# First stage with weight pieces ahead, norm chain in three pieces, gate rows into the convolution's tiles: one change to a hybrid decoder layer on one core

## Chip, cores and metric

The kernel runs on one core of a Trainium2 chip. The metric is the device time of one execution in microseconds. Engines are TensorE (PE; its weight loads are PEld), VectorE (DVE), ScalarE (ACT), GpSimd (POOL) and SyncE (SP); DMAs are issued from the queues of SP, ACT and POOL.

## What is computed

One decoder layer over 2048 tokens of width 1024, in float32, and a final RMSNorm:

```python
shift, scale, gate = split(c @ w_ada + b_ada, 3)
h = rmsnorm(x, g_pre) * (1 + scale) + shift
p = h @ w_in                       # 8 groups of 1024 columns
a = p[A_VAL] * sigmoid(p[A_GLU])
y = causal_depthwise_conv31(a, conv_w) + conv_b
y = silu(layernorm(y, conv_ln_g, conv_ln_b)) * silu(p[A_SILU])
y_a = y @ w_conv_out
u, v = gelu(p[B_U]), layernorm(gelu(p[B_V]), sgu_ln_g, sgu_ln_b)
s = per_head_causal_128x128_mix(w_s, v) + b_s
y_b = (u * s * silu(p[B_SILU])) @ w_sgu_out
merged = sigmoid(p[G_A]) * y_a + sigmoid(p[G_B]) * y_b
x = x + gate * (merged @ w_o)
out = rmsnorm(x, g_final)
```

## The kernel before

Tokens are worked in two stages of S = 1024, each in two halves of T = 512; KT = 8 tiles of 128 cover the width and NC = 4 tiles of 128 tokens a half. Float32 products are made of three matmuls: each operand is split into a first part (rounded, made by ScalarE) and a second part (the difference, made by VectorE or POOL), and first times first, first times second and second times first are added. A weight's two parts lie in a tile `whl` (5 buffers), made from a `raw` tile (8 buffers, loaded by SP). `split` (L87, L88) does it; `take` hands the pieces out in a fixed list `order` and prepares AHEAD = 4 of them. Such a piece is 128x512 in both parts; a matmul takes 128 weight columns against 512 columns.

**First stage, written by hand (L511 to L627).** Under a manual schedule each engine runs its instructions in the order written. The transposed x of the first 512 tokens is loaded into `xn`, squared on ACT (L535), summed on DVE (L536) and by TensorE (L143), and the reciprocal root, spread over all partitions by a matmul of `ones` with a diagonal (L150, L164), scales h. Then eight steps follow, one per 128 rows of the weight `w_v`. In step k TensorE runs 24 matmuls for the v columns (L592, L593, L597; the last step is L605 to L607), while for step k+1 VectorE computes the modulation (`ada`, L434), scales xn (L374), makes the second parts of two weight pieces (L88) and of h (L390), and ScalarE makes h's first part (L380) and the first parts of the weights (L87). ScalarE also squares the second half's tokens (`sx`, L585) in steps 5 and 6, takes the root (L136), loads the Gelu table by a call on one element (`warm`, L600), and evicts v (L562). In step 7 a second spread (L611) gives the second half's reciprocal root `rx1`.

The pass over the second half's v (L320 to L322) follows. From here on the tile scheduler orders instructions by priority; `run_bg(n)` puts n steps of a background list `bg` between TensorE's products at a later priority, `urgent` at the normal one, and `pause(n)` puts n empty steps in. Then come position mixing (L478), and 28 `quad`s, each a 2x2 block product of w_in in seven multiplications (L305, L308, L311). VectorE runs the convolution's taps beside them (L766, in `y` tiles of tag `x`, 8 buffers).

**Norm chain.** In background: the mean (L878), for each half eight `centre` steps (subtraction L886, square L891, adding up L895), `ln_cols` (four column sums L143, root L136, reciprocal L137), `ln_spread` (diagonal L150, matmul L164, copy to `rsq` L905). `conv_out` uses it (L941 to L944).

**Products with w_b and w_a** follow in `std_pairs`, a quarter of the columns at a time: a quarter is two halves by two columns, a product of 24 matmuls each. `done_b` multiplies by a loaded gate in its `ld` buffer (3 of them) and stores from there on POOL's queue. In the first token stage, `gate_step` (L979 to L991) loads 16 half rows of `wgate` into `raw` tiles and accumulates them on DVE in `acc`, beside the products with w_a. After these, the output product, the residual and, in the last stage, the final norm and the stores. The next stage's x is loaded (L350) into `x` tiles.

## Time and profile before

| | |
|---|---|
| runs | 1900.91, 1895.69, 1900.12 us; median 1900.12 |
| profiled execution | 1895.41 us |
| its span | 1893.7 us |
| mean granted clock of TensorE | 0.994 |
| TensorE busy | 1837.6 us, 97 %, 8104 matmuls |
| TensorE's weight loads busy | 1502.4 us, 79 % |
| VectorE busy | 1326.2 us, 70 %, 1608 instructions |
| ScalarE busy | 854.5 us, 45 % |
| GpSimd busy | 876.0 us, 46 % |
| DMA | 316.28 MB, mean 167 GB/s |

The profile is one execution, recorded by the hardware; its own time is 1895.41 us, of which the span, first to last instruction, is 1893.7. Busy times of the engines overlap. A timeline gives the start, the duration, the engine, the line, the operation with its tiles (out<-in), how many were put together (x4) and, in brackets, how long the engine had been idle before and which engine's result (or which DMA) ended that. A row whose engine ends in q is a queue's issuing work. A granted clock of 1.0 is TensorE's full level, 2.4 GHz; 0.50 is 1.2 GHz.

### The profile page before, as it was taken

To read this page: it belongs to the slowest core of one execution; us is meant where nothing else is said; L and a number is where in the kernel's file an instruction comes from. 1 tells how busy PE (TensorE), PEld (TensorE's weight loads), DVE (VectorE), ACT (ScalarE), POOL (GpSimd) and SP (SyncE) were. 2 spreads that over 40 slices of the span, in tenths; PEclk is the share of its full clock that TensorE was granted. 3 is DMA by queue.
4 is the path that set the end of the run, shared out by engine and by line. 5 is a ranking of instruction groups with operands and counts; after the bars stand their busy time and mean duration, and the time that the engine had idled before them with its cause. 6 is when DMAs were issued, how large, how long until landed. Compare 5 with 4: busy or idle time off the path is not lost.

```text
span 1893.7 us, 23201 instructions
## 1 busy us (share of the span) xinstructions
PE 1837.6 (97%) x8104; PEld 1502.4 (79%) x8104; DVE 1326.2 (70%) x1608; ACT 854.5 (45%) x1392; POOL 876.0 (46%) x734
## 2 busy tenths in 40 slices
PE   6899999999999999899999999999999999999998
PEld 4678888888888778678888888888888886888886
DVE  6887789888889854465852578778888798534424
ACT  3745455555546653222612455455555466412102
POOL 0156777777777620101100677777777776110000
PEclk9999999999999999999999999999999999999999
DMA  9673333232333277776885423233322233954494
GB/s 350 215 266 108 104 112 112 96 105 73 112 107 111 101 298 257 262 229 233 339 306 191 160 97 100 74 117 106 117 95 96 82 134 123 335 176 139 135 345 164
DMA packets 139733, 316.28 MB, mean 167 GB/s; under 512 B 15968, under 2 KB 16096, under 8 KB 139616
## 3 DMA queue, kind: packets, MB, share of 16 engines
q1 hardware_dynamic: 108576, 238.60, 37.2%
q0 software_dynamic: 11888, 41.43, 5.6%
q10 hardware_dynamic: 19152, 34.78, 4.9%
q8 instruction: 63, 1.03, 0.2%
q14 instruction: 54, 0.44, 0.1%
HBM read 229.28 MB, written 85.46 MB: 166 GB/s over the span
## 4 chain that ended last, share of the span: by engine, by line
PE 75%; issue 9%; DMA 6%; DVE 4%; ACT 2%; POOL 2%; SPq 0%; ACTq 0%; POOLq 0%; DVEq 0%
PE bank L305 22%; PE bank L311 22%; PE bank L308 22%; PE bank L320 3%; PE bank L322 3%; PE bank L321 3%; DMA raw<-in_w_v 1%; PE bank L478 1%; DMA wo<-d_wo 1%; DVE a L941 1%; DMA raw<-in_wgate 1%; ACT whl L87 1%; DMA xn<-in_xt 1%; DVE rsq L895 1%; POOL whl L88 1%
## 5 line engine op out<-in xcount | busy, mean ns | idle before, releaser
L88 POOL TENSOR_TENSOR whl<-raw,whl 128x512 fp32r<-128x512 f32 x392 | 523.4, 1340 | 339.0 <-ACT whl L87 334.2
L766 DVE SCALAR_TENSOR_TENSOR cv<-a,vec,cv 128x1024 f32<-128x1024 f32 x464 | 597.0, 1287 | 31.5 <-ACT cv L760 21.4
L87 ACT ACTIVATE whl<-raw 128x512 fp32r<-128x512 f32 x504 | 314.7, 627 | 389.2 <-PE bank L311 224.5
L311 PE MATMUL bank<-s,whl 128*128 128x512 f32 x896 | 351.9, 393 | 0.0
L305 PE MATMUL bank<-s,whl 128*128 128x512 f32 x896 | 351.5, 392 | 0.0
L308 PE MATMUL bank<-s,whl 128*128 128x512 f32 x896 | 350.1, 391 | 0.0
L232 POOL TENSOR_TENSOR raw<-raw 128x512 f32<-128x512 f32 x224 | 295.4, 1319 | 17.3
L305 PE MATMUL bank<-h,whl 128*128 128x512 f32 x672 | 264.0, 393 | 1.7 <-ACT bank L719 1.7
L308 PE MATMUL bank<-h,whl 128*128 128x512 f32 x672 | 262.4, 390 | 0.0
L311 PE MATMUL bank<-h,whl 128*128 128x512 f32 x672 | 261.7, 389 | 0.0
L311 PEld LDWEIGHTS bank<-s,whl 128*128 128x128 f32 x896 | 169.4, 189 | 36.3 <-issue 1.0
L305 PEld LDWEIGHTS bank<-s,whl 128*128 128x128 f32 x896 | 169.3, 189 | 36.4 <-issue 1.5
L308 PEld LDWEIGHTS bank<-s,whl 128*128 128x128 f32 x896 | 169.2, 189 | 35.6 <-issue 0.5
L305 PEld LDWEIGHTS bank<-h,whl 128*128 128x128 f32 x672 | 126.1, 188 | 33.8 <-DVE snap L742 5.7
L311 PEld LDWEIGHTS bank<-h,whl 128*128 128x128 f32 x672 | 126.2, 188 | 27.0 <-issue 0.5
L308 PEld LDWEIGHTS bank<-h,whl 128*128 128x128 f32 x672 | 126.2, 188 | 26.0 <-issue 0.5
L88 DVE TENSOR_TENSOR whl<-raw,whl 128x512 fp32r<-128x512 f32 x112 | 75.9, 688 | 60.0 <-ACT whl L87 59.4
L970 POOL DMA_DIRECT2D mb<-gl x32 | 17.3, 541 | 199.5 <-DVE gl L969 199.5
L714 ACT ACTIVATE snap<-bank 128x512 f32<-128x512 f32 x112 | 66.4, 597 | 94.3 <-PE bank L311 93.6
L311 PE MATMUL bank<-ya,whl 128*128 128x512 f32 x256 | 100.5, 392 | 5.4 <-DVE whl L88 5.3
L305 PE MATMUL bank<-ya,whl 128*128 128x512 f32 x256 | 100.2, 391 | 1.0 <-ACT whl L87 1.0
L305 PE MATMUL bank<-yb,whl 128*128 128x512 f32 x256 | 99.8, 390 | 1.0 <-ACT whl L87 1.0
(212 smaller groups left out, 2852.2 us busy)
## 6 DMA issues: line engine op xcount, KB each, us to landing
raw<-in_w_in SPq DMA_DIRECT2D x224, 256.0 KB, 3.0
yb<-yb SPq DMA_DIRECT2D x32, 512.0 KB, 8.0
whl<-d_wo SPq DMA_DIRECT2D x32, 512.0 KB, 4.7
whl<-d_wv SPq DMA_DIRECT2D x32, 512.0 KB, 4.2
wa<-in_wada SPq DMA_DIRECT2D x16, 512.0 KB, 7.8
raw<-in_w_v SPq DMA_DIRECT2D x32, 256.0 KB, 6.0
d_wv<-whl POOLq DMA_DIRECT2D x16, 512.0 KB, 6.6
r<-r POOLq DMA_DIRECT2D x32, 256.0 KB, 3.2
```

The costliest lines, as they stand in the source:

```text
L87: nc.scalar.activation(hi, val, AF.Copy)
L88: eng.tensor_tensor(out=lo, in0=val, in1=hi.bitcast(F32), op=ALU.subtract)
L232: eng.tensor_tensor(out=dst, in0=dst, in1=src, op=ALU.add)
L305: nc.tensor.matmul(pt, wh, h[:, 0], start=start and k == 0, stop=False, skip_group_check=True)
L308: nc.tensor.matmul(pt, wh, h[:, 1], start=False, stop=False, skip_group_check=True)
L311: nc.tensor.matmul(pt, wl, h[:, 0], start=False, stop=k == last, skip_group_check=True)
L320: nc.tensor.matmul(pt, xh, w[:, 0], start=kt == 0, stop=False)
L321: nc.tensor.matmul(pt, xh, w[:, 1], start=False, stop=False)
L322: nc.tensor.matmul(pt, xl, w[:, 0], start=False, stop=kt == KT - 1)
L478: nc.tensor.matmul(pq[:, c * P : (c + 1) * P], vn[c][:, j * P : (j + 1) * P], wsT[:, j * P : (j + 1) * P], start=c == 0, stop=True, skip_g ...
L714: nc.scalar.activation(t, pt, AF.Copy)
L766: nc.vector.scalar_tensor_tensor(out=dst, in0=a[:, k : k + S], scalar=col(V_CW, j * TAPS + k), in1=cv[0], op0=ALU.mult, op1=ALU.add,)
```

## The change

1. First loads: the first two tiles of x go on ACT's queue and the other six on SP's, in place of every second on ACT's.
2. First stage: `pieces_hi` (ACT) makes the first parts of step k+1's weights before h's first part; `pieces_lo` (DVE) makes the second parts after h's scaling. The rows of `w_v` for this pass leave `order`.
3. The squares of `sx`, the root and the Gelu table's call are issued inside the steps, ahead of h's first part; only the reciprocal and the diagonal remain behind the steps.
4. Norm chain: `ln_cols`, `ln_diag` and `ln_spread` are background steps of their own. Three `centre` steps of the second half stand ahead of the first half's sums, three between sums and diagonal, two and a pause between diagonal and spread, and pauses ahead of the second half's sums, diagonal and spread. Both stages use it.
5. `done_b` writes its product to a new t512 tile `mb`; the `ld` tile is free once read.
6. Gate rows: eight loads of whole rows (128x1024, 512 KB) on POOL's queue into `x` tiles, in which the convolution was, and eight accumulations of 128x1024 on DVE, behind a pause of 16 steps and with pauses of 2 between them. The next stage's x tiles wait for the end of the accumulation (L1154 of after; before it was for `rsq`).
7. The last stage's stores: second halves of the columns on ACT's queue, not SP's.

The diff, with unchanged lines and the pure renaming cut:

```diff
@@ -155,11 +155,10 @@
-    def spread(cols, pt=None, diag=None):
-        diag = diagonal(cols) if diag is None else diag
+    def spread(diag, pt=None):
         pt = bank() if pt is None else pt
@@ -261,7 +260,6 @@
         if s == 0:
-            order += [make_row(w_v, None, k, n) for k in range(KT) for n in range(2)]
             order += [make_row(w_v, d_wv, k, n) for n in range(2) for k in range(KT)]
@@ -512,7 +510,7 @@
         for k in range(KT):
-            (nc.scalar if k % 2 else nc.sync).dma_start(
+            (nc.scalar if k < 2 else nc.sync).dma_start(
                 out=xn[k][:, :T], in_=xt[k * P : (k + 1) * P, :T]
@@ -542,10 +540,26 @@
         ada_part(0, 0, wa[0])
-        prx = spread(rstd_cols(pc[:, :NC], NC), pc)
+        prx = spread(diagonal(rstd_cols(pc[:, :NC], NC)), pc)
         ada_part(0, 1, wa[0])
         rx = t512("rx")
-        prep_to(2)
+        pieces = {}
+        def pieces_hi(k):
+            pieces[k] = [piece_tile() for _ in range(2)]
+            for n in range(2):
+                nc.scalar.activation(pieces[k][n][:, 0], raws[id(w_v), k, n], AF.Copy)
+        def pieces_lo(k):
+            for n in range(2):
+                w = pieces[k][n]
+                nc.vector.tensor_tensor(
+                    out=w[:, 1], in0=raws.pop((id(w_v), k, n)), in1=w[:, 0].bitcast(F32),
+                    op=ALU.subtract,
+                )
+        pieces_hi(0)
+        pieces_lo(0)
         scaled(xn, prx, 0, 0)
@@ -556,6 +570,9 @@
+        def square(c):
+            nc.scalar.activation(sx[c], sx[c], AF.Square, accum_out=ssx[:, c : c + 1])
         def evict(u):
@@ -564,8 +581,7 @@
             t = A[0][k]
-            ws = [ready.pop(0) for _ in range(2)]
-            state["use"] += 2
+            ws = pieces[k]
             if k + 4 < KT:
@@ -574,17 +590,20 @@
             if k + 1 < KT:
+                pieces_hi(k + 1)
+                if k in (5, 6):
+                    square(2 * k - 10)
+                    square(2 * k - 9)
+                if k == 6:
+                    c1 = sm.tile([P, NC], F32, tag="ro", name="c1")
+                    nc.scalar.activation(c1, ssx, AF.Sqrt, bias=eps_t, scale=1.0 / D)
+                    nc.scalar.activation(warm, eps_t, AF.Gelu)
                 ada(k + 1, wa[k + 1])
...
                 h_hi(xn, 0, k + 1, A)
-                prep_to(2 * k + 4)
+                pieces_lo(k + 1)
                 h_lo(xn, 0, k + 1, A)
                 shifted(xn, 0, k + 1)
-            if k in (5, 6):
-                for c in (2 * k - 10, 2 * k - 9):
-                    nc.scalar.activation(
-                        sx[c], sx[c], AF.Square, accum_out=ssx[:, c : c + 1]
-                    )
             if k + 1 < KT:
@@ -595,9 +614,8 @@
                     nc.tensor.matmul(first[u], xl, ws[n][:, 0], start=False, stop=False)
-        c1 = rstd_cols(ssx, NC)
+        nc.vector.reciprocal(out=c1, in_=c1)
         diag1 = diagonal(c1)
-        nc.scalar.activation(warm, eps_t, AF.Gelu)
         rx1 = t512("rx1")
@@ -608,7 +626,7 @@
                 evict(1)
-                nc.scalar.activation(rx1, spread(c1, None, diag1), AF.Copy)
+                nc.scalar.activation(rx1, spread(diag1), AF.Copy)
                 scaled(xn, rx1, 1, 0)
@@ -867,6 +885,7 @@
         rcols = [None, None]
+        rdiag = [None, None]
         ya = [[None] * KT, [None] * KT]
@@ -900,8 +919,11 @@
+        def ln_diag(h):
+            rdiag[h] = diagonal(rcols[h])
         def ln_spread(h):
-            pr = spread(rcols[h], stat[0][:, half(h)])
+            pr = spread(rdiag[h], stat[0][:, half(h)])
             nc.scalar.activation(rsq[0][:, half(h)], pr, AF.Copy)
@@ -911,13 +933,19 @@
         pause(1)
-        for h in range(2):
-            bg.extend(lambda h=h, j=j: centre(h, j) for j in range(KT))
-            if h:
-                bg.append(urgent(lambda: ln_spread(0)))
-            else:
-                pause(2)
-            bg.append(urgent(lambda h=h: ln_cols(h)))
+        bg.extend(lambda j=j: centre(0, j) for j in range(KT))
+        steps = [lambda j=j: centre(1, j) for j in range(KT)]
+        bg.extend(steps[:3])
+        bg.append(urgent(lambda: ln_cols(0)))
+        bg.extend(steps[3:6])
+        bg.append(urgent(lambda: ln_diag(0)))
+        bg.extend(steps[6:])
+        pause(2)
+        bg.append(urgent(lambda: ln_spread(0)))
+        pause(2)
+        bg.append(urgent(lambda: ln_cols(1)))
+        pause(3)
+        bg.append(urgent(lambda: ln_diag(1)))
         pause(4)
@@ -965,9 +993,9 @@
         def done_b(j, h, pt):
-            g = load(d_sbg[j][h], "gl")
-            nc.vector.tensor_tensor(out=g, in0=pt, in1=g, op=ALU.mult)
-            nc.gpsimd.dma_start(out=d_mb[j][h], in_=g)
+            g, m = load(d_sbg[j][h], "gl"), t512("mb")
+            nc.vector.tensor_tensor(out=m, in0=pt, in1=g, op=ALU.mult)
+            nc.gpsimd.dma_start(out=d_mb[j][h], in_=m)
@@ -976,21 +1004,27 @@
-            def gate_step(r, n):
-                t = raw(wgate, None, wgate[r * P : (r + 1) * P, n * T : (n + 1) * T])
-                if not acc:
+            wg = []
+            for r in range(KT):
+                wg.append(xtile("wg")[:, :S])
+                nc.gpsimd.dma_start(out=wg[r], in_=wgate[r * P : (r + 1) * P, :])
+            def gate_step(r):
+                if r == 0:
                     acc.append(row("acc"))
-                v = acc[0][:, n * T : (n + 1) * T]
-                if r == 0:
                     nc.vector.tensor_scalar(
-                        out=v, in0=t, scalar1=col(V_C, r), scalar2=None, op0=ALU.mult
+                        out=acc[0], in0=wg[0], scalar1=col(V_C, 0), scalar2=None, op0=ALU.mult
                     )
...
                     nc.vector.scalar_tensor_tensor(
-                        out=v, in0=t, scalar=col(V_C, r), in1=v, op0=ALU.mult, op1=ALU.add
+                        out=acc[0], in0=wg[r], scalar=col(V_C, r), in1=acc[0],
+                        op0=ALU.mult, op1=ALU.add,
                     )
-            bg.extend(lambda r=r, n=n: gate_step(r, n) for r in range(KT) for n in range(2))
+            pause(16)
+            for r in range(KT):
+                bg.append(lambda r=r: gate_step(r))
+                pause(2)
         mg = [[None] * KT, [None] * KT]
@@ -1108,7 +1142,7 @@
                         nc.scalar.activation(o, o, AF.Copy, scale=rs)
-                    nc.sync.dma_start(
+                    (nc.scalar if n else nc.sync).dma_start(
                         out=out[t0 : t0 + P, n * T : (n + 1) * T], in_=o
@@ -1119,7 +1153,7 @@
         for k in range(KT):
-            after(xn[k][:, 0:1], rsq[0][:, 0:1])
+            after(xn[k][:, 0:1], acc[0][:, S - 1 : S])
         for h in range(2):
@@ -1128,7 +1162,7 @@
             after(r[:, 0:1], came)
-            nc.scalar.activation(r, spread(rs_next[h]), AF.Copy)
+            nc.scalar.activation(r, spread(diagonal(rs_next[h])), AF.Copy)
             rxs.append(r)
```

How the change moves instructions, at three places. In the rows, `h` is h's tile, `whl` a weight's pieces, `xn` the scaled x, `sx` the second half's tokens, `vn` the evicted v, `cols` and `c_626` the column of roots, `a` the convolution's tile (y), `rsq` the spread root, `q` a square, `zl` a loaded factor. Numbers behind names tell tiles apart; L numbers are each kernel's own.

ScalarE, from step 5 of the first stage to its first evictions, before:

```order
L380 ACTIVATE h<-xn,mod 128x512
L87 ACTIVATE whl<-raw 128x512 x2
L380 ACTIVATE xn<-xn,mod 128x512
L585 ACTIVATE sx,ssx<-sx 128x1024 x2
L380 ACTIVATE h<-xn,mod 128x512
L87 ACTIVATE whl<-raw 128x512 x5
L380 ACTIVATE xn<-xn,mod 128x512
L585 ACTIVATE sx,ssx<-sx 128x1024 x2
L136 ACTIVATE cols<-ssx,eps_t 128x4
L600 ACT_TABLE_LOAD
L600 ACTIVATE warm<-eps_t 128x1
L562 ACTIVATE vn<-bank 128x512 x2
```

and in the changed kernel:

```order
L551 ACTIVATE whl<-raw 128x512 x2
L574 ACTIVATE sx,ssx<-sx 128x1024 x2
L378 ACTIVATE h<-xn,mod 128x512
L378 ACTIVATE xn<-xn,mod 128x512
L551 ACTIVATE whl<-raw 128x512 x2
L574 ACTIVATE sx,ssx<-sx 128x1024 x2
L87 ACTIVATE whl<-raw 128x512
L599 ACTIVATE c_626<-ssx,eps_t 128x4
L600 ACT_TABLE_LOAD
L600 ACTIVATE warm<-eps_t 128x1
L378 ACTIVATE h<-xn,mod 128x512
L87 ACTIVATE whl<-raw 128x512 x2
```

Behind each pair of weight pieces (L87 before, L551 after) the squares now follow ahead of h's first part (L380, L378), and root and Gelu table (L599, L600) stand ahead of the last h instead of behind everything.

VectorE, in the pass over the second half's v, around the second part of the pass's first weights, `whl_799`, before:

```order
L390 SCALAR_TENSOR_TENSOR h_731<-xn_222,mod_86,h_731 128x512
L390 SCALAR_TENSOR_TENSOR h_736<-xn_223,mod_86,h_736 128x512
L390 SCALAR_TENSOR_TENSOR h_741<-xn_224,mod_86,h_741 128x512
L374 SCALAR_TENSOR_TENSOR xn_225<-xn_225,mod_86,rx1_666 128x512
L374 SCALAR_TENSOR_TENSOR xn_226<-xn_226,mod_86,rx1_666 128x512
L466 BN_AGGR mv_757<-st_233 128x2
L466 BN_AGGR mv_757<-st_234 128x2
L466 BN_AGGR mv_757<-st_235 128x2
L88 TENSOR_TENSOR whl_799<-raw_800,whl_799 128x512
L390 SCALAR_TENSOR_TENSOR h_746<-xn_225,mod_86,h_746 128x512
L390 SCALAR_TENSOR_TENSOR h_751<-xn_226,mod_86,h_751 128x512
```

and in the changed kernel:

```order
L372 SCALAR_TENSOR_TENSOR xn_224<-xn_224,mod_86,rx1_666 128x512
L372 SCALAR_TENSOR_TENSOR xn_225<-xn_225,mod_86,rx1_666 128x512
L372 SCALAR_TENSOR_TENSOR xn_226<-xn_226,mod_86,rx1_666 128x512
L388 SCALAR_TENSOR_TENSOR h_741<-xn_224,mod_86,h_741 128x512
L388 SCALAR_TENSOR_TENSOR h_746<-xn_225,mod_86,h_746 128x512
L388 SCALAR_TENSOR_TENSOR h_751<-xn_226,mod_86,h_751 128x512
L464 BN_AGGR mv_757<-st_233 128x2
L464 BN_AGGR mv_757<-st_234 128x2
L464 BN_AGGR mv_757<-st_235 128x2
L88 TENSOR_TENSOR whl_799<-raw_800,whl_799 128x512
L88 TENSOR_TENSOR whl_805<-raw_806,whl_805 128x512
L88 TENSOR_TENSOR whl_823<-raw_824,whl_823 128x512
```

`whl_799` stands behind the last two h's (`h_746`, `h_751`), which followed it before, and the next two second parts follow it directly.

VectorE, in the first token stage's norm chain, behind the first half's spread and up to the second spread's diagonal, before:

```order
L895 TENSOR_TENSOR rsq_5082<-rsq_5082,q_5326 128x512
L941 TENSOR_TENSOR a_1216<-a_1216,rsq_5082 128x512
L941 TENSOR_TENSOR a_1758<-a_1758,rsq_5082 128x512
L941 TENSOR_TENSOR a_2214<-a_2214,rsq_5082 128x512
L941 TENSOR_TENSOR a_2672<-a_2672,rsq_5082 128x512
L941 TENSOR_TENSOR a_3129<-a_3129,rsq_5082 128x512
L137 RECIPROCAL cols_5355<-cols_5355 128x4
L941 TENSOR_TENSOR a_3586<-a_3586,rsq_5082 128x512
L941 TENSOR_TENSOR a_4043<-a_4043,rsq_5082 128x512
L941 TENSOR_TENSOR a_4500<-a_4500,rsq_5082 128x512
L150 TENSOR_TENSOR diag_5415<-ident_80,cols_5355 128x512
L943 TENSOR_TENSOR a_1216<-a_1216,zl_5699 128x512
```

and in the changed kernel:

```order
L969 TENSOR_TENSOR a_1758<-a_1758,rsq_5082 128x512
L969 TENSOR_TENSOR a_2214<-a_2214,rsq_5082 128x512
L971 TENSOR_TENSOR a_1216<-a_1216,zl_5700 128x512
L971 TENSOR_TENSOR a_1758<-a_1758,zl_5708 128x512
L969 TENSOR_TENSOR a_2672<-a_2672,rsq_5082 128x512
L969 TENSOR_TENSOR a_3129<-a_3129,rsq_5082 128x512
L969 TENSOR_TENSOR a_3586<-a_3586,rsq_5082 128x512
L969 TENSOR_TENSOR a_4043<-a_4043,rsq_5082 128x512
L971 TENSOR_TENSOR a_2214<-a_2214,zl_5716 128x512
L969 TENSOR_TENSOR a_4500<-a_4500,rsq_5082 128x512
L137 RECIPROCAL cols_5394<-cols_5394 128x4
L150 TENSOR_TENSOR diag_5435<-ident_80,cols_5394 128x512
```

The reciprocal (L137) stood between the fifth and sixth product of y with the first half's spread (L941) and the diagonal (L150) behind all eight; now both stand behind the eighth (L969), and three products with `zl` (L971) have moved ahead of them.

## Rows read from the trace of the kernel before

**Rows 1.** What TensorE waited for: tile, line, releaser: us in total, times, longest.

```profile
PE cv L164 <- DVE diag L150: 9.4, 4, 3.0
PE bank L311 <- DVE whl L88: 5.3, 1, 5.3
PE bank L164 <- ACT vn L562: 3.3, 1, 3.3
PE bank L305 <- ACT whl L87: 2.0, 3, 1.0
...
PE bank L321 <- DVE whl L88: 1.6, 1, 1.6
...
PE bank L320 <- ACT vn L460: 1.0, 1, 1.0
```

**Rows 2.** Windows at half clock: length, PE, PEld, DVE, ACT, POOL busy, clock, DMA, GB/s.

```profile
72.40:75.80 3.40, 2.84 (x5) 1.61 (x6) 1.60 (x4) 1.72 (x5) 0.00 (x0) 0.50 1.01 381
635.60:639.00 3.40, 3.40 (x10) 2.72 (x11) 2.55 (x5) 0.26 (x1) 1.45 (x2) 0.50 0.21 74
666.30:673.10 6.80, 5.88 (x12) 3.97 (x13) 4.82 (x8) 3.30 (x6) 1.29 (x1) 0.50 0.25 77
799.40:802.80 3.40, 2.95 (x7) 2.38 (x8) 3.02 (x6) 0.00 (x0) 0.32 (x1) 0.50 0.72 240
1594.70:1598.10 3.40, 3.03 (x5) 1.81 (x6) 1.81 (x4) 0.92 (x2) 0.00 (x0) 0.50 0.30 80
```

**Rows 3.** Timeline of TensorE, first stage: start, us, engine, line, operation.

```profile
28.08 0.39 PE L592 MATMUL bank<-whl,h 128*128 128x512 f32 x1
...
31.48 0.39 PE L593 MATMUL cv<-whl,h 128*128 128x512 f32 x1
...
72.96 2.07 PE L164 MATMUL bank<-diag,ones 128*128 128x512 f32 x2 [3.35 <-ACT vn L562]
```

**Rows 4.** Timeline of VectorE, one step of the first stage.

```profile
41.19 1.22 DVE L434 CUSTOM_DVE_ANT_0 wa<-wa,cbc 128x1024 f32<-128x1024 f32 x1
...
45.92 1.29 DVE L88 TENSOR_TENSOR whl<-raw,whl 128x512 fp32r<-128x512 f32 x2 [1.31 <-ACT whl L87]
...
47.80 1.22 DVE L434 CUSTOM_DVE_ANT_0 wa<-wa,cbc 128x1024 f32<-128x1024 f32 x1
```

**Rows 5.** Timeline of ScalarE, end of the first stage.

```profile
58.48 1.14 ACT L87 ACTIVATE whl<-raw 128x512 fp32r<-128x512 f32 x2
...
69.45 1.04 ACT L585 ACTIVATE sx<-sx 128x1024 f32<-128x1024 f32 x1
...
70.92 1.28 ACT L600 ACT_TABLE_LOAD   x1
72.22 0.20 ACT L600 ACTIVATE warm<-eps_t 128x1 f32<-128x1 f32 x1
```

**Rows 6.** Timeline of VectorE, pass over the second half.

```profile
85.22 2.10 DVE L390 SCALAR_TENSOR_TENSOR h<-xn,mod,h 128x512 fp32r<-128x512 f32 x3
...
88.83 0.64 DVE L88 TENSOR_TENSOR whl<-raw,whl 128x512 fp32r<-128x512 f32 x1
```

**Rows 7.** Timeline of VectorE, norm chain, behind the first spread.

```profile
656.20 6.39 DVE L941 TENSOR_TENSOR a<-a,rsq 128x512 f32<-128x512 f32 x5 [1.25 <-ACT rsq L905]
```

**Rows 8.** Timelines of VectorE and of SyncE's queue, gate rows and next x.

```profile
797.71 0.49 DVE L985 TENSOR_SCALAR acc<-raw,vec 128x512 f32<-128x512 f32 x1 [8.64 <-DMA raw<-in_wgate]
...
889.61 0.15 DVE L92 COPY rx<-mg 128x1 f32<-128x1 f32 x1
...
786.96 3.27 SPq L350 DMA_DIRECT2D xn<-in_xt  x5
...
793.21 6.33 SPq L177 DMA_DIRECT2D raw<-in_wgate  x5
```

**Rows 9.** Window within the steps of the first stage, columns as in rows 2.

```profile
27.90:39.30 11.40, 11.23 (x50) 8.92 (x48) 8.66 (x16) 4.47 (x8) 0.00 (x0) 1.00 1.03 401
```

**Rows 10.** DMA issues: queue, number, KB each, us from issue to landing.

```profile
d_wv<-whl POOLq DMA_DIRECT2D x16, 512.0 KB, 6.6
```

## Prediction, before the change was run

> **What bounds the kernel now.** Read the busy shares first: TensorE is busy 97 % of the 1893.7 us span, VectorE 70 %. Little can come from giving other engines less to do; what can be won is time in which TensorE stands still or runs slowly. So the second view is the list of what TensorE waited for, where nearly every long entry is one place waiting for one engine [rows 1]. The third is the clock: in windows where TensorE's granted clock was 0.50, the 1.2 GHz level in place of 2.4 GHz, every busy microsecond does half a microsecond's work, so half of its busy time is lost [rows 2]. Each of these windows follows a wait of over 1.5 us or a string of column sums. The fourth is the timeline of the first stage, where no single wait is long and yet TensorE is slow: between two steps it idles in many small pieces that the waits list hardly shows [rows 3 to 5].
>
> **First stage.** In full flow a matmul takes, from start to start over 15 of them, (31.48 − 28.08)/15 = 0.2267 us [rows 3], so a step's 24 matmuls need 5.44 us. But one step lasts 47.80 − 41.19 = 6.61 us, counted on VectorE, and 1.31 us of that is VectorE waiting until ScalarE has made the first parts of the weights [rows 4]. Before, ScalarE makes them only after h's first part; now it makes them ahead of it, as the first order listing shows, and the wait should go. VectorE is then left with 6.61 − 1.31 = 5.30 us a step, just under TensorE's 5.44, so TensorE paces the steps. Step 1 begins at 28.08 [rows 3], so step 7 can begin at 28.08 + 6 × 5.44 = 60.7.
>
> The spread for the second half of tokens stands within step 7. Before, it is issued at 72.96, after a wait of 3.35 us [rows 3], because four squares of 1.04 us and the Gelu table (1.28 us) stand at the end of ScalarE's work, two squares after step 7's own pieces [rows 5]. The change puts squares, square root and table ahead of h's first part of steps 6 and 7. They are not free there: from the end of step 5 (28.08 + 5 × 5.44 = 55.3), which frees the next pieces' tiles, ScalarE must run two pieces (1.14), two squares (2.08), the root and its gap (0.4), the table (1.28) and its warming call (0.20) [rows 5], then h's first part, of a piece's size (0.57): in all 5.7 us, so h comes at about 61.0, 0.3 behind TensorE. Its second part takes VectorE about as long, seven more matmuls 1.6, and with the hand-overs the spread is issued at about 63.5. **The stage gives 72.96 − 63.5 = 9.45 us**; between 7.5 (a residue of 0.3 on each of six steps) and 10.0 (ScalarE hidden wholly).
>
> A rule speaks against putting the table into the step. The rows show the load at 70.92 for 1.28 us and the warming call at 72.22, 0.02 us behind it: the switch costs 1.3 us [rows 5]. The Trainium skill ("ScalarE: Activation LUTs", section "What ACT_TABLE_LOAD costs") adds a drain of about 1.38 us to each switch, which would put h's first part as much later and the gain at about 8.1. This trace disagrees, and I take the rows.
>
> The first loads of x, four and four on the queues of ScalarE and SyncE, become two and six. No row prices it; the nearest are SyncE's issues, from 3.27/5 = 0.65 to 6.33/5 = 1.27 us each [rows 8]. ScalarE is spared two issues and SyncE has two more, so −1.3 to +1.3; as ScalarE has the squares of these tiles to do and SyncE the loads behind, I take −0.3.
>
> **Pass over the second half.** VectorE does about 16 us of work between the spread and the second part of the pass's first weights, which before starts at 88.83 [rows 6]. The second order listing shows that piece now behind two more h's (0.70 each [rows 6]), while the step that is done before it is shorter: some +0.4 us, measured from the spread. This stretch hangs on VectorE, so the 1.42 us that the slow clock at 72.40 costs is not won: TensorE only arrives earlier, and its wait of 1.6 [rows 1] grows to 3 or 4. After such a wait I expect a new stretch of slow clock (+1.7, half of a window of 3.40 us [rows 2]; likely, not sure); the later wait of 1.0 for vn [rows 1] is covered by the delay. **Net +0.9**, between −0.8 and +2.1.
>
> **Norm chain, both stages.** TensorE waits 9.4 us in four spreads, the longest 3.0 [rows 1]. Counting rows in TensorE's order, 67 matmuls stood between the first half's sums and its spread, now 48; but squares and subtractions of the second half no longer stand between the sums and the diagonal: nine VectorE instructions at 0.64 are some 6 us, against 48 × 0.2267 = 10.9. For the second spread, 24 + 48 matmuls and two spreads of 1 us each stand after the first one, 18.3 us, where 4 + 30 stood. VectorE needs, by the third listing, eight products at 6.39/5 = 1.28 [rows 7], three more at 0.64, a reciprocal and the diagonal (0.9), with the 1.25 us of waiting ahead [rows 7] and ScalarE's copy about 15 us. Both margins hold. **−8.4**, with 1.0 kept for what is late next; ends −9.4 and −3.0. The mean's and column sums' own order costs nothing: VectorE's three earlier subtractions (1.9 us) lie under nine more matmuls (2.04).
>
> **Slow clock.** The five windows hold 2.84 + 3.40 + 5.88 + 2.95 + 3.03 = 18.10 us busy, 9.05 lost [rows 2]. Without the one counted in the pass (1.42), and with an even chance that the one behind the column sums at 635.60 stays (0.85), **−6.8**; ends −1.5 (only the one at the gate rows goes) and −9.05.
>
> **Gate rows.** Before, VectorE stands 8.64 us for a raw load of the gate weights [rows 8], and a weight's second part is queued behind it; TensorE waits 5.3 for that piece, and 2.0 for ScalarE pieces that use the same raw buffers [rows 1]. Now the rows come on POOL's queue into tiles of the convolution, ahead of use by a pause of 16 steps, in eight operations of 128x1024. **−6.3**, with 1.0 kept; ends −7.3 and, with loads that come late (below), +6.6. What is queued behind a load that waits for its tile is a store of the merge product, in POOL's queue; that product now has a buffer of its own, so the loaded one is free at its read. The next stage's loads of x, issued from 786.96 on before, now wait for the accumulations, which share their tiles; VectorE first makes a tile ready for their use at 889.61 [rows 8], four quarters later, so this costs 0. The last stores share two queues: an issue is at most 1.27, either way; I take 0.
>
> **Sum.** −0.3 − 9.45 + 0.9 − 8.4 − 6.8 − 6.3 = −30.35. The profiled execution took 1895.41; so 1865.1 for one like it. The median of the runs, 1900.12, stands 4.7 above it. I add half, 2.35: **1867 us**.
>
> **Rivals.** *Second spread stays late.* For it: products of 128x512 take 1.28 there [rows 7], twice the 0.64 of another on VectorE [rows 6], and if its other operations took as long, the margin of 3.3 us would be used up. Against it: TensorE has twice the matmuls. Two waits of 3.0 and half of their windows' 5.88 + 3.03 return: +10.5, 1877. *The loads pace the first stage.* In 27.90 to 39.30 the DMA share is 1.03 at 401 GB/s [rows 9]. A step moves 1.57 MB, 3.9 us at this pace, less than 5.44; but requests bunch. Half of the steps' gain, 4.7 us, would stay away: 1872. *Gate loads a little late*: four of the eight in file (by the next rival's prices 4 × 7.82 − 21.8 = +9.5) and two slow windows behind them (3.4): 1877 to 1880.
>
> *Slower: gate loads in single file.* Each load waits for a convolution tile, and POOL's queue is in order. A 512 KB transfer issued on it takes 6.6 us to land [rows 10]; if load and accumulation (1.22 for 128x1024 [rows 4]) alternate, a row takes 7.82 and eight 62.6 us, while the work of a quarter (four products of 24 matmuls) covers 4 × 24 × 0.2267 = 21.8. The rest, 41, would be TensorE's: 1867 + 41 = 1908. It decides from 21.8/8 = 2.7 us a row on, and reaches the old time at (33 + 21.8)/8 = 6.9. The 6.6 is a store's; no row shows such a load. Against it: the tiles come free one by one over tens of microseconds. The Trainium skill ("DMA: Bandwidth & Descriptors", section "Anatomy of one DMA — SWDGE (gpsimd) path") gives 2.0 us plus bytes at 436 GB/s, so 3.2 as an estimate; by it this rival would cost 8 × 4.42 − 21.8, about 14. No run so far shows such a load, so neither is favoured.
>
> *No change.* Every wait is replaced by an equal one behind it, since VectorE is 70 % busy and sets several of them: 1895.4 + 2.35, about 1898. The order listings speak against it.
>
> **Chances.** Forecast 0.65, second spread 0.14, load-paced 0.08, gate loads a little late 0.05, single file 0.04, no change 0.04. A measurement of this kernel can tell about 0.3 %, 5.7 us. Faster 0.92, same 0.04, slower 0.04. The range goes from 1857 (the terms near their good ends, about −38, and runs like the profiled one) to 1881 (second spread or gate loads late, and the runs as high as those shown), leaving out single file and no change.
>
> **What would show it.** Right: in the first stage VectorE waits no more for ScalarE's weights, and the spread is issued at 63 to 64; the wait for diagonals shrinks from 9.4 to about 1; the windows at 666, 799 and 1595 are gone; VectorE waits nowhere for gate rows; TensorE's wait at the second half's first pieces grows to 3 or 4 with a slow stretch behind. Wrong: a wait at the accumulations or at a POOL store behind a gate load; products that still stand ahead of the second diagonal when TensorE arrives; DMA share near 1 with VectorE waiting for ada weights.

## Result and profile after

The changed kernel takes **1875.96 us** (median of 4 runs, 1872.87 to 1876.70) against 1898.62 for the kernel before (4 runs, 1895.69 to 1900.91): a ratio of 0.9878 with a 95 % interval of 0.9859 to 0.9898, 22.7 us faster. The forecast was 1867, its range 1857 to 1881. The profiled executions are 1895.41 and 1876.56, their spans 1893.7 and 1874.8: this pair is only 18.9 us apart, because the profiled execution of before was faster than all its timed runs and that of the change is among its slowest.

TensorE runs the same 8104 matmuls in both. Its timelines give where the time came from: the start of the k-th matmul in the kernel before minus that in another kernel is what has been gained up to there. (`late_gate` and `no_load` are experiments, below.)

| up to matmul | place | after | late_gate | no_load |
|---|---|---|---|---|
| 190 | behind the first stage's spread | 9.90 | 10.60 | 10.44 |
| 500 | behind the second half's pass and mixing | 9.65 | 9.26 | 9.94 |
| 2900 | behind the first norm chain | 18.54 | 16.67 | 18.87 |
| 3300 | just behind the products with w_b | 8.80 | 18.07 | 20.48 |
| 3420 | first products with w_a | 17.45 | 26.72 | 29.13 |
| 4100 | second token stage begun | 13.64 | 21.22 | 25.41 |
| 6700 | ahead of the second norm chain | 13.57 | 21.24 | 25.33 |
| 6900 | behind it | 19.71 | 27.36 | 31.45 |
| 8103 | the last matmul | 18.84 | 26.73 | 31.01 |

The change wins where it was expected to and then loses 9.7 us in the products with w_b. What TensorE waited for in the changed kernel (tile, line, releaser: us in total, times, longest), against [rows 1]:

```profile
PE bank L303 <- ACT whl L87: 5.6, 3, 4.4
PE bank L319 <- DVE whl L88: 3.1, 1, 3.1
PE bank L318 <- DVE t L1073: 2.5, 1, 2.5
...
PE bank L309 <- DVE whl L88: 1.4, 1, 1.4
PE cv L143 <- DVE rsq L914: 1.1, 1, 1.1
```

The 9.4 us for diagonals, the 3.3 for v and the 5.3 behind a gate accumulation are not there any more. The pass over the second half waits 3.1 in place of 1.6, and two entries are new: 4.4 of the 5.6 us for a piece of ScalarE, and 2.5 for a residual product. The windows at half clock, with the columns of [rows 2]:

```profile
80.90:84.30 3.40, 3.20 (x8) 2.52 (x9) 3.40 (x8) 2.19 (x4) 2.51 (x4) 0.50 0.52 167
729.40:732.80 3.40, 3.40 (x9) 2.53 (x9) 3.38 (x9) 2.48 (x6) 0.55 (x1) 0.50 0.80 254
760.10:763.50 3.40, 3.40 (x10) 2.67 (x9) 2.44 (x5) 1.77 (x4) 0.84 (x2) 0.51 1.03 368
937.60:941.00 3.40, 3.40 (x10) 2.64 (x9) 3.40 (x7) 0.00 (x0) 0.00 (x0) 0.50 0.79 296
```

Three of the five old ones lay in the norm chains; these are gone. Each new one stands behind waits of TensorE. In the first stage, VectorE's step (the line is now L432) and TensorE's spread, which answer to [rows 4] and [rows 3]:

```profile
32.00 1.22 DVE L432 CUSTOM_DVE_ANT_0 wa<-wa,cbc 128x1024 f32<-128x1024 f32 x1
...
35.33 1.29 DVE L556 TENSOR_TENSOR whl<-raw,whl 128x512 fp32r<-128x512 f32 x2
...
37.20 1.22 DVE L432 CUSTOM_DVE_ANT_0 wa<-wa,cbc 128x1024 f32<-128x1024 f32 x1
...
64.27 1.02 PE L163 MATMUL bank<-diag,ones 128*128 128x512 f32 x2
```

A step takes VectorE 37.20 − 32.00 = 5.20 us, with no wait ahead of the second parts; TensorE's steps begin 5.44 us apart (45.31, 50.75, 56.19), and the spread stands at 64.27 with nothing waited for. ScalarE ahead of the last step:

```profile
59.59 1.28 ACT L600 ACT_TABLE_LOAD   x1
60.89 0.20 ACT L600 ACTIVATE warm<-eps_t 128x1 f32<-128x1 f32 x1
60.99 0.71 ACT L378 ACTIVATE h<-xn,mod 128x512 fp32r<-128x512 f32 x1
```

The Gelu table takes 1.28 us, the next call follows at once, and h's first part is done at 61.70, where the prediction had 61.0.

The new stall follows the matmul that starts at 724.06. ScalarE, VectorE, TensorE, SP's and POOL's queues at that place:

```profile
722.38 0.64 ACT L359 ACTIVATE xs<-xs 128x512 f32<-128x512 f32 x1 [15.00 <-DMA xs<-in_x]
...
725.40 0.63 ACT L359 ACTIVATE xs<-xs 128x512 f32<-128x512 f32 x1 [1.68 <-issue]
...
727.57 0.63 ACT L359 ACTIVATE xs<-xs 128x512 f32<-128x512 f32 x1 [1.45 <-DMA xs<-in_x]
...
728.20 0.61 ACT L87 ACTIVATE whl<-raw 128x512 fp32r<-128x512 f32 x1
...
728.85 0.69 DVE L88 TENSOR_TENSOR whl<-raw,whl 128x512 fp32r<-128x512 f32 x1 [2.52 <-ACT whl L87]
...
728.87 0.50 PE L303 MATMUL bank<-yb,whl 128*128 128x512 f32 x1 [4.42 <-ACT whl L87]
...
716.10 7.36 SPq L78 DMA_DIRECT2D xs<-in_x  x4
...
703.16 1.14 POOL L1010 DMA_DIRECT2D wg<-in_wgate  x2 [4.04 <-DVE ya L88]
...
721.04 0.54 POOL L1010 DMA_DIRECT2D wg<-in_wgate  x1 [0.64 <-DVE acc L1019]
```

ScalarE stands 15.00 us for the first load of xs (the next token stage's x, squared in background), then 1.68 us ahead of the third square, for which the profile names no cause, and 1.45 for the fourth load; only behind the fourth square does it make the weight piece at 728.20, for which VectorE (2.52 us) and TensorE (4.42) stand. The eight gate loads were issued on POOL's queue between 703.16 and 721.04. The landing times in that stretch, 703 to 730 (queue, number, KB, median us from issue to landing), in the changed kernel and then in `no_load`:

```profile
wg<-in_wgate POOLq DMA_DIRECT2D x8, 512.0 KB, 6.1
xs<-in_x SPq DMA_DIRECT2D x6, 256.0 KB, 4.8
zl<-sz SPq DMA_DIRECT2D x4, 256.0 KB, 7.5
```

```profile
xs<-in_x SPq DMA_DIRECT2D x10, 256.0 KB, 3.6
...
zl<-sz SPq DMA_DIRECT2D x4, 256.0 KB, 3.5
```

### The profile page after: what moved, and what is told of

The parts are those of the page before. It is cut to its first block, busy times and chain, and to the rows that moved or that the text cites. A ratio compares the mean times of both kernels' runs of the same rounds, so it can differ in the third digit from the quotient of the medians.

```text
span 1874.8 us, 23164 instructions
## 1 busy us (share of the span) xinstructions
PE 1831.5 (98%) x8104; PEld 1502.8 (80%) x8104; DVE 1321.1 (70%) x1600; ACT 853.9 (46%) x1392; POOL 885.3 (47%) x742
## 4 chain that ended last, share of the span: by engine, by line
PE 81%; DMA 7%; issue 5%; DVE 2%; POOL 2%; ACT 2%; SPq 0%; ACTq 0%; POOLq 0%; DVEq 0%
PE bank L303 23%; PE bank L309 23%; PE bank L306 23%; PE bank L319 3%; PE bank L320 3%; PE bank L318 3%; DMA xs<-in_x 1%; POOL whl L88 1%; DMA zl<-sz 1%; PE bank L476 1%; DMA wo<-d_wo 1%; POOL raw L231 1%; DMA whl<-d_wo 1%; PE bank L611 1%; DMA out<-xo 1%
## 5 line engine op out<-in xcount | busy, mean ns | idle before, releaser
L87 ACT ACTIVATE whl<-raw 128x512 fp32r<-128x512 f32 x488 | 305.5, 627 | 388.3 <-PE bank L309 226.2
L309 PE MATMUL bank<-s,whl 128*128 128x512 f32 x896 | 348.7, 389 | 0.0
L309 PE MATMUL bank<-h,whl 128*128 128x512 f32 x672 | 261.6, 389 | 0.0
L309 PEld LDWEIGHTS bank<-s,whl 128*128 128x128 f32 x896 | 168.1, 188 | 35.0
L309 PEld LDWEIGHTS bank<-h,whl 128*128 128x128 f32 x672 | 126.1, 188 | 26.6
L303 PE MATMUL bank<-yb,whl 128*128 128x512 f32 x256 | 101.1, 395 | 5.6 <-ACT whl L87 5.6
L1098 POOL DMA_DIRECT2D out<-xo x12 | 6.4, 534 | 207.6 <-DVE xo L1094 206.9
L309 PE MATMUL bank<-yb,whl 128*128 128x512 f32 x256 | 101.4, 396 | 1.4 <-DVE whl L88 1.4
L306 PE MATMUL bank<-yb,whl 128*128 128x512 f32 x256 | 100.7, 393 | 0.0
L309 PE MATMUL bank<-ya,whl 128*128 128x512 f32 x256 | 99.6, 389 | 0.0
```

The lines of the kernel that those rows point to most:

```text
L87: nc.scalar.activation(hi, val, AF.Copy)
L303: nc.tensor.matmul(pt, wh, h[:, 0], start=start and k == 0, stop=False, skip_group_check=True)
L306: nc.tensor.matmul(pt, wh, h[:, 1], start=False, stop=False, skip_group_check=True)
L309: nc.tensor.matmul(pt, wl, h[:, 0], start=False, stop=k == last, skip_group_check=True)
```

## Experiments

All runs of an experiment are timed beside runs of the kernel before; "faster" below is against the median of those.

**One part undone at a time.** First the whole hunk of the first stage, from the loads to the spread:

```diff
-                pieces_hi(k + 1)
...
-                pieces_lo(k + 1)
+                prep_to(2 * k + 4)
...
+        c1 = rstd_cols(ssx, NC)
```

> The changed kernel with its first stage as before (first loads, pieces, squares and table). If the first stage's gain is its own and stays (theory), the spread of the second half is again issued near 73 instead of 64.3 and the run is some 9 us slower than the change: 13 to 14 us faster than before. If that gain is given back later in any case (rival: the pass over the second half waits the longer, and later stages hang on loads and not on TensorE), the run is within 3 us of the change, some 20 to 23 faster than before.

Measured: 1885.17 against 1898.29 (0.9931, interval 0.9917 to 0.9944), 13.1 faster. The first stage is worth 22.7 − 13.1 = 9.6 us and keeps it, as the theory had it.

Then the chain's order:

```diff
-        steps = [lambda j=j: centre(1, j) for j in range(KT)]
...
+        for h in range(2):
+            bg.extend(lambda h=h, j=j: centre(h, j) for j in range(KT))
+            if h:
+                bg.append(urgent(lambda: (ln_diag(0), ln_spread(0))))
+            else:
+                pause(2)
+            bg.append(urgent(lambda h=h: ln_cols(h)))
```

> The changed kernel with the norm chain's background steps in the order of before. The four waits for diagonals (9.4 us) and their slow-clock stretches return, about 16 us over both stages. On ScalarE two squares of the next stage's tokens (xs) then stand ahead of the weight piece for which TensorE waits 4.4 us in the changed kernel, in place of four, while the gate rows are loaded as early as in the change. Theory traffic (the gate rows' 4.2 MB on POOL's queue make the loads of xs late, and ScalarE stands in front of the piece): a wait of over 2 us for a ScalarE piece stays in the products with w_b, and the run is 6 to 8 us faster than before. Theory order (the scheduler's order, with four squares ahead of the piece, makes the wait): that wait is gone, and the run is 11 to 13 us faster than before.

Measured: 1887.35 (0.9942, 0.9928 to 0.9955), 10.9 faster: the chain is worth 11.8. Its waits in the products with w_b:

```profile
PE bank L303 <- ACT whl L87: 4.4, 2, 2.7
PE bank L309 <- DVE whl L88: 3.7, 2, 3.5
```

By time the run lies at the border of the theory of order. By place the wait of 2.7 us for a ScalarE piece, with two squares ahead of the piece, speaks for traffic, but not for the gate rows' alone: it falls on matmul 3203, which waits 3.1 us in the next run too, without whole-row loads. At the matmul of the stall at 724 the wait is 1.7 in place of 4.4, which speaks for the order. The 3.5 us are VectorE's, which stands 4.39 us for a loaded factor in front of the piece. So this run alone decides nothing; `late_gate` and `no_load` do.

Then the gate rows:

```diff
-                nc.gpsimd.dma_start(out=wg[r], in_=wgate[r * P : (r + 1) * P, :])
...
+                t = raw(wgate, None, wgate[r * P : (r + 1) * P, n * T : (n + 1) * T])
...
-            after(xn[k][:, 0:1], acc[0][:, S - 1 : S])
+            after(xn[k][:, 0:1], rsq[0][:, 0:1])
```

> The changed kernel with the gate rows as before: 16 half rows on SP's queue into raw tiles during the products with w_a. The wait of about 5.3 us for a weight's second part behind a gate accumulation, with its slow clock, returns at the change from w_b to w_a (some 7 us). Theory traffic: with no gate load in the products with w_b the wait of 4.4 us and what follows it (6 us in all) is gone, and the run is within 2 us of the change, some 22 us faster than before. Theory order: three squares still stand ahead of the piece, most of the wait stays, and the run is some 16 us faster than before.

Measured: 1871.35 (0.9857, 0.9842 to 0.9872), 26.9 faster, and so 4.3 **faster than the change**. Neither theory had that. There is no stall at the 724 of the change; and the old wait of 5.3 us, which both had expected back, is not there:

```profile
PE bank L303 <- ACT whl L87: 3.1, 1, 3.1
...
PE bank L309 <- DVE whl L88: 1.3, 1, 1.3
```

So something other than the whole-row loads had removed it. The wait of 3.1 us is a later one in the products with w_b, at matmul 3203, with 6.8 us at half clock behind it. ScalarE stands for a load of xs there too, just ahead of the pieces:

```profile
749.26 0.63 ACT L359 ACTIVATE xs<-xs 128x512 f32<-128x512 f32 x1 [2.05 <-DMA xs<-in_x]
...
750.41 2.17 ACT L87 ACTIVATE whl<-raw 128x512 fp32r<-128x512 f32 x4
```

Between matmuls 2900 and 3300 this run loses 5.4 us (16.73 to 11.38), where the change loses 9.7. Its last edited line lets the next stage's x be loaded from 704 on, in the change from 724 on; that this makes xs late is not shown. The 4.3 us are thus the difference of two stalls, and the intervals of the two runs overlap.

**Gate rows later.** The edit (the last four lines stand in `done_a`; `i` counts its calls in the first token stage, `m` is the merged product):

```diff
+            def gate_load(r, m):
+                wg.append(xtile("wg")[:, :S])
+                after(wg[r][:, 0:1], m[:, 0:1])
+                nc.gpsimd.dma_start(out=wg[r], in_=wgate[r * P : (r + 1) * P, :])
...
+                if i < KT:
+                    gate_load(i, m)
+                if 2 <= i < KT + 2:
+                    bg.append(lambda r=i - 2: gate_step(r))
```

> The changed kernel with the gate rows' whole loads and their accumulations tied to the first eight products with w_a (each load waits for the merged tile of one product), so that none runs beside the products with w_b. ScalarE's order keeps four squares ahead of the piece. Theory traffic: the wait of 4.4 us in the products with w_b is gone, and none replaces it, so the run is 6 to 8 us faster than the change, 29 to 31 faster than before. Theory order: the wait stays, and the run is within 2 us of the change. Rival: the gate loads now collide with the loads of the merge factors, and TensorE waits there instead: no faster than the change.

Measured: 1868.09 (0.9844, 0.9830 to 0.9857), 30.2 faster, 7.5 more than the change. ScalarE, still with four squares ahead of the piece, now has the fourth load at 722.06, and TensorE waits for no piece in the products with w_b for over 0.2 us. As the next stage's x waits for the accumulations, its loads move too, from 724 to 818; in `no_load`, below, they stay but for one. ScalarE's squares, and the two longest waits behind the start:

```profile
716.97 0.63 ACT L359 ACTIVATE xs<-xs 128x512 f32<-128x512 f32 x1 [6.76 <-DMA xs<-in_x]
...
722.06 0.63 ACT L359 ACTIVATE xs<-xs 128x512 f32<-128x512 f32 x1 [1.11 <-DMA xs<-in_x]
...
PE bank L319 <- DVE whl L88: 3.1, 1, 3.1
PE bank L318 <- DVE t L1078: 2.8, 2, 2.2
```

**No gate loads at all.** This kernel leaves the gate rows out: the accumulations read the convolution's tiles, so the gate's values are others.

```diff
-                wg.append(xtile("wg")[:, :S])
-                nc.gpsimd.dma_start(out=wg[r], in_=wgate[r * P : (r + 1) * P, :])
+                wg.append(y[r])
```

> The changed kernel without the eight gate loads: the eight accumulations of 128x1024 stay where they were and read the convolution's tiles instead of gate rows, so the gate's input is left out and its values are others. Theory traffic: the 4.2 MB of loads alone make the wait in the products with w_b; it is gone, and the run is 5 to 8 us faster than the change, 28 to 31 faster than before. Rival accumulations: eight operations of 1.28 us on VectorE push the products that free the factor buffers, so that the xs loads are issued late; then a wait of over 2 us for a ScalarE piece stays there, and the run is within 3 us of the change.

Measured: 1867.90 against 1897.50 (0.9841, 0.9828 to 0.9855), 29.6 faster. The accumulations stayed and the stall went: traffic, not VectorE's operations. (The scheduler here put two squares ahead of the piece; that four do no harm without the loads is what `late_gate` showed.)

**Squares of the next tokens later.** These lines, moved from behind `conv_out` to behind the gate steps:

```diff
+        if not last:
+            rs_next = []
+            for h in range(2):
+                ss, sq = token_stats(s + 1, h)
+                bg.extend(sq)
+                bg.append(lambda ss=ss, h=h: rs_next.append(token_rstd(ss, f"rsn{h}")))
```

> The changed kernel with the squares of the next stage's tokens (xs, loads and ScalarE's squares) behind the gate steps in the background list, in the products with w_a; the gate rows' whole loads stay early. Theory traffic through ScalarE: what is late are the xs loads, and ScalarE, standing for them, holds up the weight piece; without xs in front of it the wait of 4.4 us is gone although the gate loads run there, and the run is 4 to 8 us faster than the change. Rival: the weights' own raw loads are late too; then a wait of over 2 us stays in the products with w_b, and the run is within 3 us of the change.

Measured: 1880.95 against 1899.80 (0.9894, 0.9879 to 0.9910), 18.9 faster, 3.8 less than the change, where the theory had 4 to 8 more. The stall in the products with w_b did go, with the gate loads where they were, which is the theory's mechanism; but two waits, with 10.2 us at half clock behind the first, came at the first output products, behind those with w_a:

```profile
PE bank L318 <- DVE m L1032: 9.6, 2, 5.0
...
860.33 0.69 DVE L88 TENSOR_TENSOR whl<-raw,whl 128x512 fp32r<-128x512 f32 x1 [4.98 <-ACT whl L87]
```

Ahead of the first of them VectorE stands 4.98 us for a weight piece, ScalarE again in front of it with the squares; ahead of the second it stands 2.88 us for a loaded factor. ScalarE, which runs its work in the given order, is the coupling: loads that its background work needs hold up the pieces behind them.

**The product's own tile.** In the kernel before, first; the second run has the reverse edit on top of `u_gate`:

```diff
-            g = load(d_sbg[j][h], "gl")
-            nc.vector.tensor_tensor(out=g, in0=pt, in1=g, op=ALU.mult)
-            nc.gpsimd.dma_start(out=d_mb[j][h], in_=g)
+            g, m = load(d_sbg[j][h], "gl"), t512("mb")
+            nc.vector.tensor_tensor(out=m, in0=pt, in1=g, op=ALU.mult)
+            nc.gpsimd.dma_start(out=d_mb[j][h], in_=m)
```

> The kernel before with one edit: the product of the w_b stage goes into a tile of its own, so that its loaded factor is free once read. Theory own tile: the wait of 5.3 us before the gate accumulations came from SP's queue, which stood for a free factor buffer with the gate loads behind it; with the edit alone it is gone or under 1.5 us, and the run is 4 to 8 us faster than before. Rival chain: the wait is gone in the kernel without the whole-row loads because the norm chain brings VectorE's products forward; then it stays here, and the run is within 2 us of before.

Measured: 1891.13 (0.9949, 0.9933 to 0.9966), 8.7 faster, from one tile. SP's queue in the kernel before, with three factor loads ahead of the run of gate loads:

```profile
778.02 5.76 SPq L78 DMA_DIRECT2D gl<-sbg  x3
```

and SP's queue and VectorE with the edit, to be held against this row and [rows 8]:

```profile
767.85 3.31 SPq L78 DMA_DIRECT2D gl<-sbg  x3
...
782.15 1.05 SPq L177 DMA_DIRECT2D raw<-in_wgate  x2
...
789.96 0.49 DVE L985 TENSOR_SCALAR acc<-raw,vec 128x512 f32<-128x512 f32 x1 [6.32 <-DMA raw<-in_wgate]
...
791.37 0.68 DVE L88 TENSOR_TENSOR whl<-raw,whl 128x512 fp32r<-128x512 f32 x1
```

The run of gate loads begins at 782.15 in place of 793.21, the accumulation that VectorE stands for at 789.96 in place of 797.71 (it still stands 6.32 us, but early enough), and the piece behind it is done at 792, where TensorE needs it at 796. So the wait that the prediction put down to the raw loads was made by SP's queue standing for a factor buffer.

> The changed kernel with the gate rows as before and the w_b product back in its loaded factor's buffer. Theory own tile: the wait of 5.3 us for a weight's second part behind a gate accumulation returns, with a slow-clock stretch, and the run is 5 to 8 us slower than the one with the gate rows alone undone, some 20 us faster than before. Rival chain: it doesn't return, and the run is within 2 us of that one, 26 to 28 us faster than before.

Measured: 1877.19 (0.9881, 0.9864 to 0.9897), 22.6 faster, 4.3 less than with the gate rows alone undone. The time agrees better with the theory than with its rival:

```profile
PE bank L303 <- ACT whl L87: 6.8, 2, 4.7
...
PE bank L309 <- DVE whl L88: 0.7, 1, 0.7
```

TensorE has no wait of 5 us behind an accumulation, but one of 4.7 for a ScalarE piece at matmul 3203, where it waited 3.1 in `u_gate`. VectorE's stand for the raw load, however, is back, 9.48 us against 2.27 in `u_gate` and 8.64 in the kernel before:

```profile
782.13 0.49 DVE L1013 TENSOR_SCALAR acc<-raw,vec 128x512 f32<-128x512 f32 x1 [9.48 <-DMA raw<-in_wgate]
```

The piece behind it costs TensorE only 0.7 us (the L309 row), as TensorE itself had just been held up. So the own tile cuts VectorE's stand with the chain changed too; why ScalarE's piece comes later than in `u_gate` is open.

**Second parts on POOL.** On top of `late_gate`, in `make_row`:

```diff
-            split(w, raws.pop((id(mat), k, n)))
+            split(w, raws.pop((id(mat), k, n)), nc.gpsimd if cache is d_wv and n == 0 else nc.vector)
```

> The changed kernel with the gate rows tied to the products with w_a, as in the earlier run, and the second parts of the first eight weights of the second half's pass made on POOL, which is idle there, in place of VectorE. Theory: the wait of 3.1 us in that pass is set by VectorE's order, with the second part behind eight h's; it is gone, and the slow clock behind it too, so the run is 4 to 6 us faster than with the gate rows tied alone: 34 to 36 us faster than before. Rival: the first parts on ScalarE or the raw loads come as late; then a wait of 2 us or more stays there, and the run is within 2 us of the one with the gate rows tied alone.

Measured: 1866.39 (0.9827, 0.9809 to 0.9845), 33.4 faster: the fastest of all, though its lead of 1.7 us over `late_gate` is within what the runs scatter (3.2 when each is held against its own runs of before; the theory had 4 to 6). The theory falls in the main point:

```profile
77.81 0.73 PE L320 MATMUL bank<-whl,h 128*128 128x512 f32 x2 [3.64 <-DVE h L388]
```

The wait for weights is gone and one of 3.64 us for h's second part has taken its place. In both orders VectorE's work for the second half sets the end there.

**Both kernels profiled again,** without an edit.

> The changed kernel once more, unaltered, for a second look at the wait of 2.5 us in the output products of the first token stage, where VectorE and ScalarE stand for the stores of finished tokens (8.2 us to land in the first look, 6.5 in the kernel before, with the same order of issue). Theory: the wait is this kernel's own and shows again at 2 us or more. Rival: it is chance of one execution, and is under 1.5 us here.

> The kernel before once more, unaltered, for a second look at the same place: the wait for the residual product was 0.3 us there, and the stores landed in 6.5 us. Theory: it stays under 1 us. Rival (chance of one execution): it is 1.5 us or more here, and the execution is some 3 us longer than the one profiled first.

Measured: the residual's wait is 2.6 us again in the changed kernel (1872.98 in all), and 1.7 in the kernel before (1901.42). For the changed kernel the theory holds; for the one before the rival does, and its wait lies at 0.3 in one execution and 1.7 in the other. The stores landed in 8.6 and 7.2 us. In this second execution of the changed kernel the wait of 3.1 us in the pass over the second half was there and no slow window behind it; the stall for ScalarE's piece was 4.2 us, the loss between matmuls 2900 and 3300 8.2 (20.04 to 11.89).

## Why the prediction was right in sign and range, and short by 9 us

The profiled pair's 18.84 us stand against the forecast's 30.35, term by term from the table:

| term | forecast | measured |
|---|---|---|
| first loads and first stage | 9.75 | 9.90 |
| pass over the second half | −0.9 | −0.25 |
| both norm chains, with their share of the slow clock | 13.7 | 8.9 + 6.1 = 15.0 |
| gate rows, with the slow clock behind them | 7.8 | 18.54 to 17.45, −1.1 |
| output products of the first token stage | 0 | −3.8 |
| the rest | 0 | −0.9 |

(13.7 is 8.4 and the slow clock's 6.8 without the gate rows' 1.48; 7.8 is 6.3 and that 1.48.)

**Right.** The steps of the first stage are paced by TensorE; the spread was forecast at about 63.5 and stands at 64.27. The squares and the Gelu table were not free, and TensorE waits a little for them, as worked out. That 9.90 meets 9.75 is partly luck: at the spread itself the gain is 72.96 − 64.27 = 8.69, and the rest comes in the next three matmuls, which in the kernel before lay in the slow window at 72.40 that the forecast did not count as won. The pass over the second half waits 3.1, forecast 3 to 4, and a slow window follows in most executions, not in all.

The chain's two margins held: no wait for a diagonal is left in them. They are wider than worked out, by something the prediction did not have. It priced VectorE's products at 1.28 us each, a mean of two kinds (first token stage, before and changed kernel; ns, least, median and most):

```profile
L941 DVE TENSOR_TENSOR a<-a,rsq x16: 677/1722/1782, 656.2 to 683.4; 128x512 f32<-128x512 f32 x16
L969 DVE TENSOR_TENSOR a<-a,rsq x16: 676/684/1787, 642.9 to 670.3; 128x512 f32<-128x512 f32 x16
```

Each of those that last 1.7 to 1.8 us, in both kernels and both token stages, begins while an operation of POOL's runs on 128x512 tiles. In the changed kernel only one of the first half's eight is long, in place of five; that they now come where POOL has less to do is luck.

**Wrong: the step "gate rows".** The old wait is gone and brought 8.65 us (8.80 to 17.45 in the table), near the 7.8 of the sum; missing from the sum are the 9.74 lost just ahead of it (18.54 to 8.80). The step took the old wait for the price of 16 raw loads and credited its removal to the new way of loading. Two runs show otherwise. The own tile alone, which the prediction named in one sentence and priced at nothing, wins 8.7 us. And the whole-row loads win nothing on top of it: without them the run is 4.3 faster by medians, and by place the two profiled executions of the change do 4.4 and 2.8 us worse than `u_gate` from matmul 2900 to 3420. The prediction asked who is queued behind the loads on POOL's queue and on VectorE; it did not ask what the loads take from transfers on other queues. It also has the next stage's x issued from 786.96 on; that is the second half of it, and the first eight loads were issued from 723.84 on, in the products with w_b, where SP's queue carries xs too. Its rival "gate loads a little late" had the place nearly right and the mechanism wrong: VectorE's accumulations do stand for loads, but it is ScalarE, for xs, that TensorE waits for. So that the time still lies within the range is in part luck: the upper end was set for gate loads that hold up VectorE and for a late second spread, and neither came.

**Not foreseen: the output products.** TensorE's wait of 2.5 us there, with a slow window, belongs to no single part of the diff: it is 1.1 us with the first stage or the chain undone, and 1.8 to 2.8 in the other runs that have both. VectorE and ScalarE stand for the stores of finished tokens, which land in 8.2 to 8.6 us in two executions of the changed kernel, 6.5 and 7.2 in the kernel before, with stores and weight loads issued at the same distances. In `late_gate` they land in 6.6 and the wait is still 2.2, so the landing is not the whole of it. The cause is open.

By medians the parts nearly close: first stage 9.6, chain 11.8, own tile 8.7 and gate loads −4.3 make 25.8, where the whole is 22.7. They need not add up, since a wait that one part removes may be hidden by another.

## What to carry over

When a wait goes through a queue, ask what that queue stood for before: here a buffer held by a store, two steps upstream of the load that the engine was seen waiting for, and one tile cured it. A load moved to another queue and to an earlier time made the loads of another queue land later here (7.5 us in place of 3.5); look at who loads in that stretch, and at the in-order engine that mixes background work with pieces that the bottleneck needs. Counting the bottleneck engine's instructions and subtracting start times in two traces shows within minutes where a gain was won and where it was given back.

## What the runs showed of the hardware

With 4.2 MB on POOL's queue beside them, loads of 256 KB on SP's queue took 7.5 us (zl) and 4.8 (xs) to land in the median, against 3.5 and 3.6 without; a 512 KB load on POOL's queue took 6.1, close to the 6.6 of a store in [rows 10]. The formula of the Trainium skill ("DMA: Bandwidth & Descriptors", section "Anatomy of one DMA — SWDGE (gpsimd) path") gives 3.2 as an estimate; the measurement, taken in this traffic, decides. Stretches at the 1.2 GHz level do not follow from a wait alone: the same wait of 3.1 us was followed by none, by 3.4 us and by 6.8 us of half clock in different executions. VectorE's products of two 128x512 tiles in the norm chains took 0.68 us or 1.7 to 1.8, and all of the latter (18 before, 8 in the changed kernel) began while an operation of POOL's ran; where three of 0.68 us ran beside one of POOL's (from 646.25, and again from 1571.82), POOL's took 3.3 us, where half of its operations of that size took under 1.3. Why is not shown.
